# A decoder layer on one core: half of two transposed operands made by VectorE and DMAs, output projection by column halves

## The chip, the core and the metric

The kernel runs on one NeuronCore of a Trainium2 chip. A core has a matrix engine (TensorE, PE in the profile; its weight loads are PEld), VectorE (DVE), ScalarE (ACT), GpSimd (POOL) and SyncE (SP, which issues nearly all DMAs here), each with its own queue of instructions that run in order. The engines wait for each other through semaphores. The metric is the device time of one execution in microseconds.

## What is computed

One layer of a hybrid decoder on an input of 256 tokens by 1024 channels, float32, DEPTH and BATCH 1. Cut to what matters here:

```python
h = rmsnorm(x, norm1_g); u = h @ w_in            # split into x_rnn, g_rnn, q, k, v, g_br
ya = rg_lru(causal_dwconv(x_rnn)) * gelu(g_rnn)  # recurrent branch
yb = moba_attention(q, k, v)                     # 8 heads of 128; with 256 tokens: one causal block
gates = sigmoid(g_br)
merged = gates[0] * (ya @ w_proj_rnn) + gates[1] * (yb @ w_proj_attn)     # "the gated sum"
x = x + merged @ w_out
h = rmsnorm(x, norm2_g)
act = gelu(causal_dwconv(h @ w_up)) * (h @ w_gate)
x = x + act @ w_down
```

The products are made with three matmuls each: every operand is split into a high part (rounded to fp32r) and a low part (the rest), and hi*hi + hi*lo + lo*hi is summed in PSUM.

## The kernel before

**Weights as a stream.** All weights come as chunks of 128x2048 float32 (1 MB). `load_next` (L378) issues a chunk's DMA on SP into one of three raw buffers; `advance` (L401) loads up to three chunks ahead and has ScalarE make the high part (`hi`) and VectorE the low part (`lo`) with `split_part` (L397). For the chunks in `DVE_HI` (39, 42 and 43) VectorE makes both.

**Units.** `UNITS` (L34) lists the units of the first half of the layer. A unit takes one chunk: 4 quarters of 6 matmuls (`tm_mm`, L683: 2 halves of the tokens, 3 products), for half of the contraction and 512 output columns. So a pair of units, such as pa0 and pa1, makes 512 columns of one product, and the second one ends with the evacuation from PSUM. pr are the units of ya @ w_proj_rnn, pa of yb @ w_proj_attn, ga and gb of the gates. `pr_evac` (L843) multiplies with the gate, `pa_evac` (L847) multiplies and adds: half g (512 columns) of the gated sum then stands in `sgb`, tokens on the partitions.

**Transposes.** A product needs its stationary operand with the contraction on the partitions. `m_t` (L853) turns a quarter of the gated sum with four TensorE transposes (128x128, fp32) into PSUM and splits it into `mh`, `ml`; the four calls are the items m0 to m3. `norm2_t` (L949) does the same for a quarter of the updated x (one half of the tokens, one half of the columns; items n00, n10, n01, n11), multiplies with norm2_g and splits into `h2h`, `h2l`; it also sums the squares. The other way to transpose is `turn` (L437): VectorE transposes blocks of 32x32 within its partitions, four DMAs write the blocks to DRAM in the order in which they are to come back, and a fifth DMA, issued later as an item of its own, reads them. It is used for q, k, the recurrent branch and the FFN's up and gate products.

**Output projection.** `out_proj` (L968) uses `wout` in chunks of 256 rows by all 1024 columns; for each column half it runs over chunks, tokens and the two row blocks of a chunk (`rows_mm`, L933), 96 matmuls in four PSUM banks, and `norm2` (L945) adds the result to x in `xs`.

**FFN.** Blocks of 512 columns in pairs p = 0 to 4: `pair_half` (L1071) is a unit of 24 matmuls for up or gate and one half (kh) of the contraction. At the end of the second half the product is turned; `pair_up` and `pair_gate` work on it, and `downs` runs the down projection two pairs later. Pair 0's units come in the order up00, gt00, up01, gt01 (kind, pair, half of the contraction), the others' in the order up, up, gate, gate.

**The order.** Nothing is scheduled by the compiler. `AFTER` (L36) says after which quarter of which unit each item is put down. What the functions put down is kept in two lists, one for TensorE and one for all other engines, and `ORDER` (L161), a string written out in full, interleaves them: `+3` means the next three TensorE instructions, `157` the instruction with that number of the other list. The order of TensorE is fixed by the units; the order on every other queue, SP's too, by `ORDER`. Buffers are given out along this order (`Pool`, L245).

Of the kernel before, what the change touches and what calls it, by code (L numbers as in the profile page):

```python
# [14 lines left out]
P = 128  # L15
S = 256
D = 1024
KT = D // P
# [16 lines left out]
         "gb1 gb2 gb3 pr0 pr1 pr2 pr3 pa0 pa1 pa2 pa3")  # L35
# [65 lines left out]
    "pr2.1": "s36",  # L101
    "pr2.2": "O6",
    "pr2.3": "O0",
    "pr3.0": "s37",
    "pr3.3": "sb1",
    "pa1.0": "O7",
    "pa2.1": "m0",
    "pa3.2": "s38",
    "wo.0": "s39 m1",
    "wo.4": "m2",  # L110
    "wo.5": "s40",
    "wo.6": "m3",
    "wo.12": "n00",
    "wo.13": "n10",
    "wo.14": "s41",
    "up00.0": "s42 n01",
    "up00.2": "n11",
    "gt00.0": "s43",
    "gt00.3": "s44",
    "up01.3": "s45 s46",  # L120
    "gt01.2": "s47",
    "gt01.3": "bcast2",
    "up10.0": "ur0 s48",
    "up10.1": "s49",
    "up11.0": "s50",
    "up11.2": "fu0",
    "gt10.0": "s51",
    "gt10.1": "s52 gr0",
# [33 lines left out]
0-2 +1 3-4 +1 5 +1 6 +1 8 +1 7 +1 9 +1 11 +2 10 25 +1 12 30 +1 26-27 +1 14 +1 28 33 +1 29 +1 13 31 +2 32 +2 34 +1  # L162
35 +3 15 +7 36 +2 41 +3 19 +3 37 63 +1 42 +1 39 +3 43 +1 40 +1 17 38 +3 44 +1 49 +2 18 +3 45 64 50 +1 47 +4 51 46
+2 16 48 +3 52 +1 57 +4 53 +1 58 +1 55 +4 59 54 +2 56 +3 60 +7 66 +4 68 +1 67 +5 69 +3 99 +3 65 +5 70 100 +5 71 +5
72 +1 98 73 +1 74 +1 75 +1 76 +1 77 +1 78 104 +1 79-80 +1 81 +1 82 +1 83 +4 84 +1 105 +2 85 +4 116 +4 86 +1 103 +3
# [6 lines left out]
+6 188 228 +1 235 +4 189 +1 308 +2 242 190 +3 191 +2 162 240 +1 192 243 +2 244 247 +1 248 193 239 +1 249-250 +1  # L172
245 251 +2 246 +1 252 271 +2 272 +1 253 +1 229 +2 254 232 +1 309 +2 233 255 +2 230 +1 256 +2 322 +1 257 +2 231 +1
258 307 +2 234 +1 259 +3 260 273 +1 274-275 +1 276 108 261 +3 262 297 +2 323 +1 109 +1 263 329 +2 110 +3 277 +1
111 +3 112 +1 278 +6 299 279 +1 301 +1 321 +3 280 +2 332 330 +2 281 +3 282 +3 283 312 +2 311 302 +1 284 328 314 +2
264 313 305 285 +2 316 303 265 +1 286 315 +1 304 +1 317 +1 266 306 287 +1 318 +1 118 +1 288 +2 333 267 347 +1 289
+1 268 +2 194 269 +3 195 +2 298 196 +3 197 +1 300 +1 270 +1 198 +1 354 331 +1 355-356 +1 357 291 358 +3 290 359
# [8 lines left out]
+3 472 +1 391 +1 428 392 +1 393 +1 476 +3 478 +7 466 +1 473-474 467 +1 439 +2 468 +3 469 +1 527 470 +2 471 +5 484  # L186
+3 485 +2 479 +1 492 +3 494 +2 499 +6 486 528 +1 477 +3 496 +2 429 497 +2 537 +2 487 +1 539 +4 500 +3 507 +9 540
+1 502 498 +1 488 +1 503 +2 210 +1 489 +1 490-491 +2 431 +6 493 432 +4 495 +4 509 +2 510 +3 532 508 +12 504 538 +1
# [8 lines left out]
639 +3 655 +1 657 +9 668 653 +1 669-670 +1 671 +1 672 +1 673 +1 674 +1 675 +1 676 +1 658 +1 660 +9 677 +1 656 678  # L197
# [16 lines left out]
937 +1 936 +2 939 +1 938 +2 940-942  # L214
"""


class Ref:


    def __init__(self, make, root=None):
        self.make, self.made, self.root = make, None, root or self

# [76 lines left out]
def trunk_layer(ctx: ExitStack, tc: tile.TileContext, xT, x, vec, win_fm, win_tm, wri, wpr, wpa,  # L300
# [47 lines left out]
    def two(w, base, c):  # L348
# [7 lines left out]
              "pr": lambda c: two(wpr, 0, c), "pa": lambda c: two(wpa, 0, c)}  # L356
    units = [(u[:-1], int(u[-1])) for u in UNITS.split()]
    chunk = {u: add(source[u[0]](u[1])) for u in units}
    c_wo = [add(wout[c]) for c in range(4)]

    NP = NF // 2
    c_up, c_gt, c_dn = {}, {}, []
# [838 lines left out]
```

## Time and profile before

| | |
|---|---|
| median of 3 runs | 435.13 us (435.06 to 435.16) |
| the profiled execution | 435.01 us, its span 433.2 us |
| TensorE busy | 428.4 us (99%), 2044 instructions, granted clock 1.000 |
| VectorE, ScalarE, GpSimd busy | 326.8 (75%), 256.9 (59%), 50.1 us (12%) |
| DMA | 100.06 MB, mean 231 GB/s |

The span runs from the first to the last instruction; the rest of the profiled execution's time lies around it. In the profile's slices (40 equal parts of the span) a digit is a busy share in tenths. All operations carry line 296 (L296), the line at which the recorded list is issued, so the rows are told apart by their tiles: `mT` and `h2T` are the TensorE transposes of the gated sum and of x, `yo` the output projection, `sgb`, `xs`, `mh`, `ml`, `h2h`, `h2l` as above, `acc` the down projection, and names such as `fupd`, `gtm`, `gm`, `qm` are the SBUF and DRAM tiles of turns. "DMA to landing" is the time from the issue on SP to the last byte's semaphore.

### The profile page before, as it was taken

How to read it: one execution, taken by the hardware profiler on the slowest of the kernel's cores; microseconds unless marked ns; L12 is line 12 of the kernel's file. 1: busy time of each engine (PE TensorE's matmuls, PEld its weight loads, DVE VectorE, ACT ScalarE, POOL GpSimd, SP SyncE). 2: the span in 40 equal slices, each digit the busy share in tenths (PEclk: the TensorE clock that was granted, in tenths of full speed). 3: DMA queues.
4: the chain of work that ended last, by engine and by line, in shares of the span. 5: the costliest groups of instructions: out<-in, count | busy, mean ns of one | idle time of the engine just before them, and what ended most of it. 6: DMA issues, size and time to landing. Idle time of an engine off the chain costs nothing.

```text
span 433.2 us, 5466 instructions
## 1 busy us (share of the span) xinstructions
PE 428.4 (99%) x2044; PEld 360.0 (83%) x2044; DVE 326.8 (75%) x426; ACT 256.9 (59%) x285; POOL 50.1 (12%) x101
## 2 busy tenths in 40 slices
PE   8999999999999999999999999999999999999996
PEld 8888888888888888888888888888888888888985
DVE  3877499799888898985666896496979766767643
ACT  4687596886779999963431453357455555355410
POOL 0021007767660000000000000000000000000000
PEclk9999999999999999999999999999999999999999
DMA  7998944889991752274454466888789787697202
GB/s 259 404 385 243 360 153 147 269 292 326 372 358 52 276 194 97 98 290 130 163 194 141 151 220 202 288 288 300 238 264 328 256 285 245 211 317 249 97 2 97
DMA packets 32826, 100.06 MB, mean 231 GB/s; under 512 B 3104, under 2 KB 13472, under 8 KB 29088
## 3 DMA queue, kind: packets, MB, share of 16 engines
q1 hardware_dynamic: 32656, 99.71, 67.1%
q8 instruction: 16, 0.26, 0.2%
q14 instruction: 10, 0.08, 0.1%
q10 hardware_dynamic: 144, 0.00, 0.0%
HBM read 89.22 MB, written 10.49 MB: 230 GB/s over the span
## 4 chain that ended last, share of the span: by engine, by line
PE 97%; DMA 1%; DVE 0%; SPq 0%; ACT 0%; issue 0%
PE acc L296 14%; PE up L296 13%; PE gt L296 13%; PE pr L296 5%; PE gb L296 5%; PE yo L296 5%; PE ga L296 5%; PE v L296 5%; PE pa L296 5%; PE q L296 5%; PE k L296 5%; PE rg L296 5%; PE rx L296 4%; DMA raws<-in_win_fm 1%; PE gtl L296 1%; PE upl L296 1%
## 5 line engine op out<-in xcount | busy, mean ns | idle before, releaser
L296 DVE TENSOR_TENSOR lo<-raw,hi 128x2048 fp32r<-128x2048 f32 (+1 forms) x72 | 160.0, 2224 | 27.2 <-issue 9.5
L296 ACT CAST hi<-raw 128x2048 fp32r<-128x2048 f32 (+1 forms) x69 | 128.4, 1863 | 87.0 <-PE up L296 11.5
L296 PE MATMUL up<-hi,h2h 128*128 128x512 f32 x80 | 31.4, 393 | 0.0
L296 PE MATMUL up<-hi,h2l 128*128 128x512 f32 x80 | 31.1, 389 | 0.0
L296 PE MATMUL acc<-hi,fah 128*128 128x512 f32 x80 | 31.1, 389 | 0.0
L296 PE MATMUL acc<-lo,fah 128*128 128x512 f32 x80 | 31.1, 389 | 0.0
L296 PE MATMUL gt<-hi,h2l 128*128 128x512 f32 x80 | 31.1, 389 | 0.0
L296 PE MATMUL gt<-hi,h2h 128*128 128x512 f32 x80 | 31.1, 389 | 0.0
L296 PE MATMUL gt<-lo,h2h 128*128 128x512 f32 x80 | 31.1, 389 | 0.0
L296 PE MATMUL acc<-hi,fal 128*128 128x512 f32 x80 | 31.1, 389 | 0.0
L296 PE MATMUL up<-lo,h2h 128*128 128x512 f32 x80 | 31.1, 389 | 0.0
L296 ACT ACT_TABLE_LOAD x14 | 18.0, 1283 | 3.1 <-PEq L1191 1.2
L296 DVE SCALAR_TENSOR_TENSOR fc<-fu,pv,fc 128x255 f32<-128x255 f32 (+1 forms) x40 | 17.0, 475 | 2.0 <-ACT fc L296 1.9
L296 POOL TENSOR_TENSOR rsq<-rsq 128x8 f32<-128x8 f32 x32 | 17.1, 533 | 11.8 <-DVE rsq L296 9.6
L296 PEld LDWEIGHTS acc<-hi,fal 128*128 128x128 f32 x80 | 15.0, 188 | 3.2
L296 PEld LDWEIGHTS gt<-hi,h2h 128*128 128x128 f32 x80 | 15.0, 188 | 3.1
L296 PEld LDWEIGHTS up<-hi,h2l 128*128 128x128 f32 x80 | 15.0, 188 | 3.1
L296 PEld LDWEIGHTS acc<-hi,fah 128*128 128x128 f32 x80 | 15.0, 188 | 3.1
L296 PEld LDWEIGHTS gt<-lo,h2h 128*128 128x128 f32 x80 | 15.0, 188 | 3.1
L296 PEld LDWEIGHTS gt<-hi,h2l 128*128 128x128 f32 x80 | 15.0, 188 | 3.1
L296 PEld LDWEIGHTS up<-hi,h2h 128*128 128x128 f32 x80 | 15.0, 188 | 3.0
L296 PEld LDWEIGHTS acc<-lo,fah 128*128 128x128 f32 x80 | 15.0, 188 | 3.0
(228 smaller groups left out, 1041.3 us busy)
## 6 DMA issues: line engine op xcount, KB each, us to landing
raw<-in_win_fm SPq DMA_DIRECT2D x12, 1024.0 KB, 7.6
raw<-in_win_tm SPq DMA_DIRECT2D x12, 1024.0 KB, 6.2
raw<-in_wup SPq DMA_DIRECT2D x11, 1024.0 KB, 5.5
raw<-in_wgate SPq DMA_DIRECT2D x11, 1024.0 KB, 7.7
raw<-in_wdown SPq DMA_DIRECT2D x11, 1024.0 KB, 7.0
raw<-in_wpr SPq DMA_DIRECT2D x4, 1024.0 KB, 4.9
raw<-in_wpa SPq DMA_DIRECT2D x4, 1024.0 KB, 4.9
raw<-in_wout SPq DMA_DIRECT2D x4, 1024.0 KB, 4.8
```

The lines of the kernel that those rows point to most:

```text
L296: getattr(engine, name)(*map(real, a), **{n: real(v) for n, v in k.items()})
```

## The change

- Half 0 of the gated sum (columns 0 to 511) is turned with `turn` in place of m0 and m1: items mt (one VectorE transpose of 128x1024 and four writes), mr (the read), ms (cast and low part). m2 and m3 stay on TensorE.
- Half 1 of x for norm2 is turned in place of n01 and n11: ht (two VectorE transposes, four writes), hr (the read), hs (four ScalarE scalings by norm2_g, cast, low part, squares). n00 and n10 stay on TensorE.
- The output projection becomes four units wo0 to wo3 like the others: wo0 and wo1 make columns 0 to 511 over the whole contraction, wo2 and wo3 the rest. Each chunk is loaded by two DMAs of 512 KB.
- pa0 and pa1 run before pr3 (pr2, pa0, pa1, pr3, pa2, pa3), so half 0 of the gated sum is complete while three more units are left before wo0. Items of attention (O0, O6, O7) move with them.
- In the FFN the first units come as up00, gt00, up10, up01, gt01, up11, gt10, gt11: three units use half 0 of norm2's output before up01 needs half 1. Pair 1's products use the other PSUM pool.
- `ORDER` is written anew from near the start on, 958 numbers in place of 943 and 2015 TensorE instructions in place of 2031.

```diff
-         "gb1 gb2 gb3 pr0 pr1 pr2 pr3 pa0 pa1 pa2 pa3")
+         "gb1 gb2 gb3 pr0 pr1 pr2 pa0 pa1 pr3 pa2 pa3 wo0 wo1 wo2 wo3")
...
-    "pa1.0": "O7",
-    "pa2.1": "m0",
+    "pa0.0": "O6",
+    "pa0.2": "O7",
+    "pa1.0": "s37",
+    "pa1.3": "mt sb1",
+    "pr3.2": "mr",
+    "pa2.3": "ms",
...
-    "wo.0": "s39 m1",
-    "wo.4": "m2",
...
-    "wo.6": "m3",
-    "wo.12": "n00",
-    "wo.13": "n10",
...
-    "up00.0": "s42 n01",
-    "up00.2": "n11",
...
+    "wo0.1": "m2",
+    "wo0.2": "m3",
...
+    "wo2.0": "n00 s41",
+    "wo2.1": "n10",
+    "up00.0": "s42 ht",
+    "up00.3": "s43 hr",
+    "gt00.2": "hs",
...
+    def by_columns(w, c):
+
+        cs = slice(c // 2 * 512, c // 2 * 512 + 512)
+        return [w[2 * (c % 2) + j].rearrange("p (k c) -> p k c", k=2)[:, :, cs] for j in range(2)]
...
+            return [(n[:2], int(n[2]), int(n[3])) for n in "up00 gt00 up10 up01 gt01 up11 gt10 gt11".split()]
+        return [(kind, p, kh) for kind in ("up", "gt") for kh in range(2) if p > 1]
...
+    def m_turn():
+
+        turn("mm", turned_m, sgb.half(0), "mr")
...
+    def m_split():
+        v = lambda a: a.half(0).rearrange("p (u i b) -> p u i b", u=8, i=4)
+        split2(v(mh), v(ml), by_tile(turned_m))
+
+    def m_stat(a, k, t):
+        return head_q(a, k, t) if k < 4 else a[k][:, t * P:(t + 1) * P]
...
+    def norm2(hf, ps):
+        for t in range(2):
+            nc.vector.tensor_add(xs[:, t, halves[hf]], ps[t], xs[:, t, halves[hf]])
+
+    def squares(t, hf):
+        nc.scalar.activation(small(f"sq2{t}{hf}", 512), xs[:, t, halves[hf]], AF.Square,
+                             accum_out=ss2[:, hf, t:t + 1])
...
+    def h2_turn():
+        turn("hm", turned_h, [xs[:, t, halves[1]] for t in range(2)], "hr")
+
+    def h2_split():
+        m = half("h2p")
+        for k in range(4):
+            d = turned_h.rearrange("p (i t c b) -> p c t i b", i=4, t=2, c=4)[:, k]
+            nc.scalar.activation(kt(m)[:, k, :].rearrange("p (t i b) -> p t i b", t=2, i=4), d, AF.Copy,
+                                 scale=pv[:, V_G2 + 4 + k:V_G2 + 5 + k])
+        split2(h2h.half(1), h2l.half(1), m)
+        for t in range(2):
+            squares(t, 1)
...
-            open_ps[kind, p] = [bank(f"{kind}{p}{t}") for t in range(2)]
+            open_ps[kind, p] = [psA.tile([P, 512], F32, tag="A", name=f"{kind}{p}{t}") if p == 1 else bank(f"{kind}{p}{t}")
+                                 for t in range(2)]
```

More of the change, by code (lines that the diff above doesn't have):

```diff
@@ L100 @@
     "pr2.0": "P6",
[L101 to L105, printed above, removed]
-    "pa1.0": "O7",
-    "pa2.1": "m0",
-    "pa3.2": "s38",
-    "wo.0": "s39 m1",
-    "wo.4": "m2",
-    "wo.5": "s40",
-    "wo.6": "m3",
-    "wo.12": "n00",
-    "wo.13": "n10",
-    "wo.14": "s41",
-    "up00.0": "s42 n01",
-    "up00.2": "n11",
[L118 to L128, printed above, removed]
+    "pr2.1": "s36 O0",
+    "pa0.0": "O6",
[4 more added lines that the diff above has]
+    "pa2.3": "ms",
+    "pa3.2": "s38",
+    "wo0.0": "s39",
+    "wo0.1": "m2",
+    "wo0.2": "m3",
+    "wo1.0": "s40",
+    "wo2.0": "n00 s41",
[3 more added lines that the diff above has]
+    "gt00.2": "hs",
+    "up10.0": "s44 s45",
+    "up01.0": "s46 bcast2",
+    "gt01.0": "s47",
+    "up11.0": "s48 ur0",
+    "gt10.0": "s49 s50",
+    "gt10.2": "s51 fu0",
+    "gt11.0": "s52 gr0",
     "gt11.1": "ur1",
@@ L161 @@
 ORDER = """
[L162 to L165, printed above, removed]
[6 rows of a table removed]
-+6 188 228 +1 235 +4 189 +1 308 +2 242 190 +3 191 +2 162 240 +1 192 243 +2 244 247 +1 248 193 239 +1 249-250 +1
@@ L173 @@
[L173 to L177, printed above, removed]
[8 rows of a table removed]
@@ L186 @@
-+3 472 +1 391 +1 428 392 +1 393 +1 476 +3 478 +7 466 +1 473-474 467 +1 439 +2 468 +3 469 +1 527 470 +2 471 +5 484
-+3 485 +2 479 +1 492 +3 494 +2 499 +6 486 528 +1 477 +3 496 +2 429 497 +2 537 +2 487 +1 539 +4 500 +3 507 +9 540
-+1 502 498 +1 488 +1 503 +2 210 +1 489 +1 490-491 +2 431 +6 493 432 +4 495 +4 509 +2 510 +3 532 508 +12 504 538 +1
[8 rows of a table removed]
-639 +3 655 +1 657 +9 668 653 +1 669-670 +1 671 +1 672 +1 673 +1 674 +1 675 +1 676 +1 658 +1 660 +9 677 +1 656 678
[16 rows of a table removed]
-937 +1 936 +2 939 +1 938 +2 940-942
+0-2 +1 3-4 +1 5 +1 6 +1 8 +1 7 +1 9 +1 11 +2 10 25 +1 12 30 +1 26-27 +1 14 +1 28 33 +1 29 +1 13 31 +2 32 +2 34 +2
@@ new lines @@
+35 +3 15 +6 36 +3 41 +3 19 +2 37 +1 63 42 +1 39 +4 43 38 +1 17 +1 40 +3 44 +1 49 +4 45 64 +1 50 +1 47 18 +3 51 +1
+46 +1 16 +1 48 +2 52 +2 57 +4 53 +1 58 +1 55 +3 59 +1 54 +1 56 +3 60 +8 66 +4 68 67 +6 69 +2 99 +3 65 +5 70 +1 100
++10 104 98 +8 71 105 +10 72 +1 103 73 +1 116 74 +1 75 +1 76 +1 77-78 +1 79 +1 80 +1 81 +1 82 +2 117 +3 61 137 +4
[7 rows of a table added]
++1 235 +3 204 +2 308 +2 242 +1 205 +4 247 206 240 +1 248 239 +1 249-250 +1 243 251 +1 244 +2 252 245 +2 246 +1 253
[4 rows of a table added]
++2 270 +1 209 +3 298 +3 300 +3 331 +1 354 +1 355-356 +1 357 290 358 +3 291 359 326 +2 348 +1 320 360 327 +3 350
[8 rows of a table added]
@@ L215 @@
+392 +1 393 +1 469 +1 470-471 +2 472 538 +1 210 +3 473 +3 484 +3 485 +2 479 +2 492 +2 494 +3 499 +5 486 539 +1 477
[10 rows of a table added]
+671-672 +1 673 +1 674 664 +1 666 +8 650 +1 675 +1 659 676 +1 677 662 +1 678 +1 679 +1 680 +1 681-682 +8 667 +4 651
[16 rows of a table added]
+952 +1 951 +2 954 +1 953 +2 955-957
 """
@@ L355, in trunk_layer, with ffn_order @@
               "ga": lambda c: two(win_fm, 8, c), "gb": lambda c: two(win_fm, 12, c),
-              "pr": lambda c: two(wpr, 0, c), "pa": lambda c: two(wpa, 0, c)}
+              "pr": lambda c: two(wpr, 0, c), "pa": lambda c: two(wpa, 0, c), "wo": lambda c: by_columns(wout, c)}
     units = [(u[:-1], int(u[-1])) for u in UNITS.split()]
     chunk = {u: add(source[u[0]](u[1])) for u in units}
-    c_wo = [add(wout[c]) for c in range(4)]
     NP = NF // 2
+    def ffn_order(p):
+        if p == 0:
+            return [(n[:2], int(n[2]), int(n[3])) for n in "up00 gt00 up10 up01 gt01 up11 gt10 gt11".split()]
+        return [(kind, p, kh) for kind in ("up", "gt") for kh in range(2) if p > 1]
     c_up, c_gt, c_dn = {}, {}, []
     for p in range(NP):
-        for c, kh in ((c_up, 0), (c_gt, 0), (c_up, 1), (c_gt, 1)) if p == 0 else (
-                (c_up, 0), (c_up, 1), (c_gt, 0), (c_gt, 1)):
+        for kind, p, kh in ffn_order(p):
+            c = c_up if kind == "up" else c_gt
             c[p, kh] = add(two(wup if c is c_up else wgate, 0, 2 * p + kh))
@@ L381, in load_next @@
         raw[i] = wp.tile([P, 2048], F32, tag="raw", name=f"raw{i}")
+        if isinstance(stream[i], list):
+            n = 2048 // len(stream[i])
+            for a, src in enumerate(stream[i]):
+                d = raw[i][:, a * n:(a + 1) * n]
+                nc.sync.dma_start(d.rearrange("p (k c) -> p k c", k=2) if len(src.shape) == 3 else d, src)
+            return
         if len(stream[i].shape) == 3:
@@ L405, in advance @@
             j = split_tiles()
-            n, m = min(2048, stream[j].shape[-1] * (2 if len(stream[j].shape) == 3 else 1)), {4: 2}.get(j, 1)
+            src = stream[j]
+            n = 2048 if isinstance(src, list) else min(2048, src.shape[-1] * (2 if len(src.shape) == 3 else 1))
+            m = {4: 2}.get(j, 1)
             for a in range(m):
@@ L681, in trunk_layer, with tm_mm @@
     ybh, ybl = Act("ybh", F32R), Act("ybl", F32R)
-    def tm_mm(ps, i, k, k4, ah, al, split=False):
+    def tm_mm(ps, i, k, k4, ah, al, split=False, stat=lambda a, k, t: a[k][:, t * P:(t + 1) * P]):
         at = (lambda a: a.rearrange("p (c k n) -> p k c n", c=2, k=4)[:, k4]) if split else (
@@ L688, in tm_mm @@
         for t in range(2):
-            ts = slice(t * P, (t + 1) * P)
             o = ps[t].rearrange("p (c n) -> p c n", c=2) if split else ps[t]
-            mm3(o, ah[k][:, ts], al[k][:, ts], at(hi[i]), at(lo[i]), k == 0, k == KT - 1)
+            mm3(o, stat(ah, k, t), stat(al, k, t), at(hi[i]), at(lo[i]), k == 0, k == KT - 1)
     SC = P ** -0.5
@@ L851, in pa_evac, with by_tile @@
             nc.vector.tensor_add(m, m, tok(sga, g, t))
+    turned_m = half("md")
+    def m_turn():
+        turn("mm", turned_m, sgb.half(0), "mr")
+    def by_tile(d):
+        return d.rearrange("p (i u b) -> p u i b", u=8, i=4)
+    def m_split():
[3 more added lines that the diff above has]
+        return head_q(a, k, t) if k < 4 else a[k][:, t * P:(t + 1) * P]
     def m_t(c):
@@ L862, in trunk_layer @@
     evac = {"rg": rg_ps.__setitem__, "v": v_evac, "pr": pr_evac, "pa": pa_evac, "ga": lambda g, ps: gate_evac(sga, g, ps),
-            "gb": lambda g, ps: gate_evac(sgb, g, ps)}
+            "gb": lambda g, ps: gate_evac(sgb, g, ps), "wo": lambda g, ps: norm2(g, ps)}
     def run_unit(kind, c):
@@ L897, in run_unit @@
             for k4 in range(4):
-                tm_mm(ps, i, 4 * kh + k4, k4, *{"pr": (yah, yal), "pa": (ybh, ybl)}.get(kind, (xgh, xgl)),
-                      kind not in "qkv")
+                tm_mm(ps, i, 4 * kh + k4, k4, *{"pr": (yah, yal), "pa": (ybh, ybl), "wo": (mh, ml)}.get(kind, (xgh, xgl)),
+                      kind not in ("q", "k", "v", "wo"), *((m_stat,) if kind == "wo" else ()))
                 if kh and k4 == 3:
@@ L917, in trunk_layer @@
             item[f"{n}{h}"] = lambda fn=fn, h=h: fn(h)
-    for n in range(4):
+    for n in (2, 3):
         item[f"m{n}"] = lambda n=n: m_t(n)
+    item["mt"], item["ms"] = m_turn, m_split
     def run(name, quarters):
@@ L925, in run @@
                 advance(int(n[1:])) if n[1:].isdigit() and n[0] == "s" else item[n]()
-    yo = {}
     h2h, h2l = Act("h2h", F32R), Act("h2l", F32R)
@@ L943, in trunk_layer @@
     rs2 = const.tile([P, 2], F32, name="rs2")
-    def norm2(t, hf):
-        cs = halves[hf]
-        nc.vector.tensor_add(xs[:, t, cs], yo[t, hf], xs[:, t, cs])
+    def norm2(hf, ps):
[4 more added lines that the diff above has]
+                             accum_out=ss2[:, hf, t:t + 1])
+    turned_h = half("hd")
+    def h2_turn():
[9 more added lines that the diff above has]
+            squares(t, 1)
     def norm2_t(t, hf):
@@ L958, in norm2_t @@
         split2(kt(h2h.half(hf))[:, :, ts], kt(h2l.half(hf))[:, :, ts], m)
-        nc.scalar.activation(small(f"sq2{t}{hf}", 512), xs[:, t, halves[hf]], AF.Square,
-                             accum_out=ss2[:, hf, t:t + 1])
-    def wo(j, t, hf):
-        advance(c_wo[j])
-        if j == 0:
-            yo[t, hf] = psA.tile([P, 512], F32, tag="A", name=f"yo{t}{hf}")
-        rows_mm(yo[t, hf], c_wo[j], mh.pair(j), ml.pair(j), t, halves[hf], j == 0, j == 3)
-    def out_proj():
-        for hf in range(2):
-            for j in (0, 1):
-                for t in range(2):
-                    wo(j, t, hf)
-                    yield
-        for hf in range(2):
-            for t in range(2):
-                wo(2, t, hf)
-                yield
-                wo(3, t, hf)
-                norm2(t, hf)
-                yield
+        squares(t, hf)
     for t in range(2):
-        for hf in range(2):
-            item[f"n{t}{hf}"] = lambda t=t, hf=hf: norm2_t(t, hf)
+        item[f"n{t}0"] = lambda t=t: norm2_t(t, 0)
+    item["ht"], item["hs"] = h2_turn, h2_split
     for kind, c in units:
@@ L987, in trunk_layer @@
             run(f"{kind}{c}", run_unit(kind, c))
-    run("wo", out_proj())
     rbf = const.tile([P, S], F32, name="rbf")
@@ L1067, in trunk_layer @@
         item[f"fg{p}"] = lambda p=p: pair_gate(p)
-    item["n11"] = lambda: norm2_t(1, 1)
     item["bcast2"] = norm2_bcast
@@ L1107, in trunk_layer @@
     for p in range(NP):
-        for kind, kh in (("up", 0), ("gt", 0), ("up", 1), ("gt", 1)) if p == 0 else (
-                ("up", 0), ("up", 1), ("gt", 0), ("gt", 1)):
-            run(f"{kind}{p}{kh}", pair_half(kind, p, kh))
+        for kind, n, kh in ffn_order(p):
+            run(f"{kind}{n}{kh}", pair_half(kind, n, kh))
         if p >= 2:
```

83 rows, old and new, of the table ORDER are left out of this document.

## The prediction

> **What bounds the kernel now.** I read the page first: its shares, its slices and the chain that ended last.
>
> ```profile
> span 433.2 us, 5466 instructions
> ...
> PE 428.4 (99%) x2044; PEld 360.0 (83%) x2044; DVE 326.8 (75%) x426; ACT 256.9 (59%) x285; POOL 50.1 (12%) x101
> ...
> PE   8999999999999999999999999999999999999996
> ...
> DMA  7998944889991752274454466888789787697202
> ...
> PE 97%; DMA 1%; DVE 0%; SPq 0%; ACT 0%; issue 0%
> ```
>
> TensorE is busy in 9 tenths or more of every slice but the first and the last, and 97% of the chain is TensorE. The view of TensorE's waits says how little is lost to others:
>
> ```profile
> PE warm L296 <- DVE ones L296: 1.0, 1, 1.0
> PE rx L296 <- ACT his L296: 0.2, 1, 0.2
> ```
>
> 1.2 us, both before the stream is running. So from about 10 us on the time is the sum of TensorE's instructions. Removing one saves what it takes in the queue; any new wait of TensorE is added in full. The chain in order of time (start, length, what) gives these prices:
>
> ```profile
> 225.35 0.44 PE mT L296 x4
> ...
> 249.47 0.44 PE h2T L296 x4
> 249.90 2.74 PE up L296 x12
> 252.65 0.44 PE h2T L296 x4
> 253.08 1.38 PE up L296 x6
> 254.46 5.44 PE gt L296 x24
> ```
>
> A group of four transposes takes 0.44 us; a unit (24 matmuls with 512 columns) takes 5.44 us, 0.227 us per matmul. Quoted are three of the four groups that the change removes (m1, n01, n11); m0's takes the same.
>
> **The change part by part.**
>
> *Transposes removed from TensorE:* 4 groups x 0.44 = 1.76 us. The matmul after a group starts some hundredths late as well (249.90 with 12 matmuls takes 2.74, against 12 x 0.2267 = 2.72), so I take 0.45 a group: 1.80 us. All of it is on the path. Listed singly, a transpose is longer:
>
> ```profile
> L296 PE MATMUL h2T<-ident,xs 128*128 128x128 f32 x16 | 2.4, 272 | 0.0
> ```
>
> 272 ns is the time of one from start to end (mT's are the same), and they overlap: 0.44/4 = 0.11 us each is what they hold the queue for, and that is what I take. [...]
>
> *Output projection by column halves:* 4 units of 24 matmuls, 96 as before, of the same shape. Nothing on TensorE. Its loads become 8 of 512 KB instead of 4 of 1024 KB: four more issues on SP. In the new order each such load stands 87 to 117 matmuls (20 to 27 us) ahead of use, against 4.8 us from issue to landing now:
>
> ```profile
> raw<-in_wout SPq DMA_DIRECT2D x4, 1024.0 KB, 4.8
> ```
>
> No gain is possible, and a load four times as slow would still be in time: nothing.
>
> *The work of the two turns.* Durations, VectorE first, then ScalarE:
>
> ```profile
> L296 DVE STREAM_TRANSPOSE qd<-q 128x512 f32<-128x512 f32 x4 | 2.7, 698 | 0.0
> L296 DVE TENSOR_TENSOR h2l<-h,h2h 128x512 fp32r<-128x512 f32 x4 | 2.7, 690 | 0.9 <-ACT h2h L296 0.7
> ...
> L296 DVE STREAM_TRANSPOSE kd<-kr 128x1024 f32<-128x1024 f32 x2 | 2.5, 1242 | 0.0
> ...
> L296 DVE TENSOR_TENSOR qTl<-qd,qTh 128x1024 fp32r<-128x1024 f32 x2 | 2.5, 1232 | 1.1 <-ACT qTh L296 1.1
> ```
>
> ```profile
> L296 ACT ACTIVATE fc<-fu,pv 128x256 f32<-128x256 f32 x20 | 10.7, 593 | 6.2 <-DVE fu L296 6.2
> ...
> L296 ACT ACTIVATE qTh<-qd 128x1024 fp32r<-128x1024 f32 x2 | 2.1, 1046 | 0.0
> ```
>
> VectorE loses six instructions of 128x512 (two each of ml, h and h2l), 6 x 0.69 = 4.1 us, and gets 1.24 + 2 x 0.70 (transposes) + 2 x 1.23 (low parts) = 5.1 us; ScalarE gets 4 x 0.59 + 2 x 1.05 for four casts of about 0.6, some 2 us more. VectorE is 75% busy, so one more microsecond is covered. What matters is the latency: VectorE transposes, four DMAs write to DRAM, one reads back, then ScalarE and VectorE split. The nearest rows for an uncrowded round trip (issues on SP; then KB and us to landing, each from its own window):
>
> ```profile
> 86.17 1.78 SPq L296 DMA_DIRECT2D gm<-gr  x4
> ```
>
> ```profile
> gm<-gr SPq DMA_DIRECT2D x4, 128.0 KB, 2.4
> ```
>
> ```profile
> raw<-in_wri SPq DMA_DIRECT2D x1, 512.0 KB, 3.2
> ```
>
> Last write issued about 1.4 us after the first, landed 2.4 later, then a 512 KB read of 3.2: 7.1 us with a little for semaphores. The crowded end is the FFN:
>
> ```profile
> 268.25 2.39 SPq L296 DMA_DIRECT2D upm<-fupd  x4
> ```
>
> ```profile
> upm<-fupd SPq DMA_DIRECT2D x4, 128.0 KB, 5.7
> ```
>
> ```profile
> fupd<-upm SPq DMA_DIRECT2D x1, 512.0 KB, 6.3
> ```
>
> Some 1.8 us between first and last issue, 5.7 and 6.3: 13.8 us. I take 7.1 for both new turns, because in the new order the last weight load stands 16 to 28 matmuls (4 to 6 us) ahead of the writes, near its landing, and the next one behind the read.
>
> *First turn (half of the gated sum).* Call T0 the end of unit pa1. How long the sum takes after it, from VectorE's timeline:
>
> ```profile
> 211.97 1.37 DVE L296 TENSOR_TENSOR sgb<-pa,sgb 128x512 f32<-128x512 f32 x2 [2.65 <-PE pa L296]
> 213.26 1.28 DVE L296 TENSOR_TENSOR sgb<-sgb,sga 128x512 f32<-128x512 f32 x2
> ```
>
> It ends at 214.54. The chain, in the same stretch:
>
> ```profile
> 208.45 6.89 PE pa L296 x30
> ```
>
> The first 18 of these 30 are the end of pa1, so pa1 ended near 212.6: the sum is there at T0+1.9. Transposed T0+3.1, landed T0+10.3. The order puts two low-part splits, two multiplies and the cast and low part of wo1 on VectorE in between; at about 2.3, 0.7, 1.2 and 2.3 us they run until T0+12.5, so the low part is ready by T0+13.7. TensorE has three units (pr3, pa2, pa3) before wo0: T0+16.3, and wants the low part at the third matmul, T0+16.8. Spare: 3.1 us. At the crowded price it would be ready at T0+19.5: a stall of 2.7 us. Behind the waiting cast stand ScalarE's casts of wo2 and wo3, behind the waiting read SP's loads of the same chunks, used two units later.
>
> *Second turn (half of norm2's input).* T1 is the end of wo3. The last addition into xs ends at about T1+0.9, the two transposes at T1+2.3, the round trip at T1+9.5 (SP can issue at once: its load of gt01 is issued before T1, when VectorE has split gt00). Then four scalings, cast and low part: 2.4 + 1.05 + 1.23 and 0.2 of semaphores = 4.9, ready T1+14.4. Between lie three units (up00, gt00, up10): up01 starts at T1+16.3 and wants the low part at 16.8. Spare: 2.4 us; crowded price: a stall of 4.3 us. Behind the waiting first scaling stands ScalarE's cast for up11, and behind the waiting read SP's loads of up11 and gt10; they are due two to four units later.
>
> *Attention units inside the recurrent branch's, pair 1 opened early, the written order renewed.* The count of matmuls for attention is the same. In the stretch of the projections the low parts of the weights stand 34 to 69 matmuls ahead of use in the new order, 19 to 63 before (wo1 apart): easier. P6 and O0 stay well ahead of pa0 (the last low part of yb0 10 matmuls, 2.3 us, for a 0.42 us instruction). PSUM: pair 1 uses the four banks that wo frees. Cost nothing; bounds, by the 0.2 us wait at the start that could vanish or double, and by a few hundredths where transposes of attention change neighbours: -0.2 to +0.3 us.
>
> **Sum.** The profiled execution took 435.01 us, 1.8 of it outside its span; minus 1.80 gives 433.2. The median of the runs is 0.12 higher: 433.3 us.
>
> **The rivals.**
>
> *A turn comes late (the other side).* If the second round trip is crowded like the FFN's, TensorE waits 4.3 us at up01.0: 435.1 - 1.8 + 4.3 = 437.6 us. It decides from a round trip of 9.5 us on (stall begins) and 11.3 us (gain gone). For it: the quoted read of 6.3 us, which shared the queue with weights and other turns. Against: DMA is at 4 to 6 tenths here (the 19th to 24th slice), at 6 to 9 in the FFN. [...] Chance 0.11.
>
> *Half late.* A crowded write (7.5) with a free read (3.2) is 10.7 us, a stall of 1.2 us: 434.5, within 0.2% of before. Chance 0.10.
>
> *The FFN's DMA burst.* In the new order up of pair 0, gate of pair 0 and up of pair 1 finish in three units running (now two, and the third after a gap), so 1 MB more crowds the queue at one place. Tightest today, VectorE's timeline and the chain:
>
> ```profile
> 367.25 2.29 DVE L296 TENSOR_TENSOR lo<-raw,hi 128x2048 fp32r<-128x2048 f32 x1
> ```
>
> ```profile
> 369.18 10.88 PE gt L296 x48
> ```
>
> The low part ends at 369.54 and its unit starts at 374.6: 5.1 us spare where SP has already been held up. A megabyte more is about 3.2 us: twice the difference between the quoted 4.8 for 1024 KB and 3.2 for 512 KB. Covered; if not, a stall of 1 to 2 us, 434.3 to 435.3. Chance 0.04, half of it slower or same.
>
> *Each transpose holds TensorE for its listed 272 ns:* 16 x 0.272 = 4.35 us, 430.8. The chain speaks against. 0.02.
>
> *The removed time does not come back* because what follows was waiting anyway: the waits view shows none. In the same 0.10 as half late.
>
> **How the numbers follow.** Clean gain 0.73, with its own range 432.9 to 433.8 (the bounds above). 0.2% is 0.87 us, about what a measurement tells from no change. Faster (below 434.26): 0.73 + 0.02 + 0.02 = 0.77; same 0.10 + 0.01 = 0.11; slower 0.12. Range 432.7 to 435.2: up to where the gain is just lost, which leaves out the late turn and the 272 ns case.
>
> **What would show it.** Right: TensorE's waits still two lines before 11 us; the chain without mT before pa's last unit and with two h2T groups; wo in units of 5.44 us; the first scaling behind the turn on ScalarE ends several microseconds before up of pair 0 starts its second half. Wrong: a wait of PE wo on the low part of the gated sum, or of PE up on h2l; a wait of PE on lo anywhere in the FFN; the round trips longer than 9.5 us.

## The result and the profile after

| | before | after |
|---|---|---|
| median | 435.15 us (434.94 to 435.6, 8 runs) | 437.18 us (434.93 to 438.63, 8 runs) |
| profiled execution, its span | 435.01, 433.2 us | 438.48, 436.7 us |
| TensorE busy, instructions | 428.4 us, 2044 | 428.0 us, 2028 |
| ScalarE busy, table loads | 256.9 us, 14 | 262.0 us, 17 |

The changed kernel is slower: 1.0046 times the time of before, interval 1.0032 to 1.0061, some 2.0 us. Forecast were 433.3 us, a gain of 1.8. Sixteen TensorE instructions are gone, and TensorE's busy time has hardly fallen. The page of after shows the place. In the lines with slices each digit is a fortieth of the span, 10.9 us.

```profile
span 436.7 us, 5470 instructions
...
PE 428.0 (98%) x2028; PEld 359.7 (82%) x2028; DVE 328.8 (75%) x425; ACT 262.0 (60%) x290; POOL 50.3 (12%) x101
...
PE   8999999999988999999999999999999999999996
...
PEclk9999999999998999999999999999999999999999
...
PE 86%; DMA 6%; ACT 4%; DVE 2%; issue 1%; SPq 0%; ACTq 0%
```

Two slices of TensorE show an 8 in the middle of the kernel (the 12th and 13th, 120 to 142 us), the granted clock dips in the 13th, and the chain that ended last, 97% TensorE before, now runs 14% of the way through other engines. The place is the attention stage, 80 us ahead of the first of the new turns. TensorE's waits (in all, times, longest) name the wait:

```profile
PE pt L293 <- DVE sm L293: 3.5, 1, 3.5
PE warm L293 <- DVE ones L293: 1.0, 1, 1.0
PE rx L293 <- ACT his L293: 0.8, 1, 0.8
```

`pt` are the TensorE transposes of a head's softmax `sm`; this is the first head that is worked on. The chain in order of time shows what they waited for:

```profile
131.04 1.18 ACT sm L293 x4
...
132.44 0.30 DVE sm L293
...
132.88 0.88 PE pt L293 x3
133.75 6.52 PE ga L293 x24
```

ScalarE's exponentials came late, and VectorE scaled them at once. Behind the wait, 24 matmuls of `ga` took 6.52 us. The windows of that stretch (length, then busy time and count for each engine, granted clock, DMA share, GB/s) show why:

```profile
128.50:133.00 4.50, 1.01 (x8) 0.80 (x7) 2.05 (x8) 4.47 (x9) 1.87 (x6) 0.94 0.79 252
133.00:136.50 3.50, 3.50 (x12) 2.88 (x13) 3.33 (x9) 3.50 (x7) 0.00 (x0) 0.59 0.70 253
```

For 3.5 us after the wait the granted clock is 0.59: a loss of 3.5 x 0.41 = 1.4 us more, with which the idle time is paid for a second time. "Busy" hides it, since slow matmuls count as busy.

**The balance.** The first `pt` transposes start at 132.88, against 128.84 before:

```profile
128.84 0.33 PE pt L296 x3
129.17 5.51 PE ga L296 x24
```

That is 4.04 us late, some 0.5 of it from the start of the kernel (the wait of `rx` for the first weights, 0.8 against 0.2 us in the waits view) and the rest from the wait. The 0.5 is not the work of the new order: the first load took 6.69 us in place of 6.19, and the two orders are the same up to TensorE's 20th instruction. In the runs below the wait of `rx` was anything from none (old front) to 1.0 us (casts of q and k back). At the lower clock the transposes take 0.88 in place of 0.33 and the matmuls 6.52 in place of 5.51, together 1.6 us. That makes 5.6 us, and from there on nothing is lost. At the end of the changed stretch (gate of pair 0; before it began at 254.46, a row of the prediction) the lag is 258.13 - 254.46 = 3.67 us:

```profile
242.22 0.44 PE h2T L293 x4
...
252.69 5.44 PE up L293 x24
258.13 5.44 PE gt L293 x24
263.57 6.81 PE up L293 x30
```

So 0.5 + 3.5 + 1.6 us came in ahead, and 5.6 - 3.7 = 1.9 us were taken off in the stretch where the four groups of transposes stood. The gain came as forecast; it is hidden by a loss elsewhere. The mean granted clock was 0.999 or 1.000 in three of the eight runs (434.93 to 436.13 us) and 0.992 to 0.996 in the other five (437.17 to 438.63 us), so the second payment is not made in every execution.

**Why the exponentials were late.** ScalarE before, from its timeline (start, length, instruction, in brackets the idle time ahead of it and what ended it):

```profile
121.25 1.06 ACT L296 ACTIVATE tt<-rt 128x1024 f32<-128x1024 f32 x1 [2.12 <-DVE rt L296]
123.19 1.28 ACT L296 ACT_TABLE_LOAD   x1 [0.87 <-DVE mx L296]
124.48 0.49 ACT L296 ACTIVATE sm<-sm,mx,rq 128x128 f32<-128x128 f32 x1
```

and after:

```profile
111.53 1.06 ACT L293 ACTIVATE qTh<-qd 128x1024 fp32r<-128x1024 f32 x1 [5.25 <-DMA qd<-qm]
...
113.88 1.90 ACT L293 CAST hi<-raw 128x2048 fp32r<-128x2048 f32 x1
...
119.04 1.28 ACT L293 ACT_TABLE_LOAD   x1
120.33 1.06 ACT L293 ACTIVATE rt<-rt 128x1024 f32<-128x1024 f32 x1
121.43 1.06 ACT L293 ACTIVATE a<-rt 128x1024 f32<-128x1024 f32 x1
122.39 1.04 ACT L293 ACTIVATE tt<-rt 128x1024 f32<-128x1024 f32 x1
123.47 1.06 ACT L293 ACTIVATE rt<-rt 128x1024 f32<-128x1024 f32 x1
...
127.38 1.28 ACT L293 ACT_TABLE_LOAD   x1
128.68 1.06 ACT L293 ACTIVATE tt<-tt 128x1024 f32<-128x1024 f32 x1
129.74 1.28 ACT L293 ACT_TABLE_LOAD   x1
131.04 0.49 ACT L293 ACTIVATE sm<-sm,mx,rq 128x128 f32<-128x128 f32 x1
```

Before, ScalarE idles for 0.87 us and is there when the softmax's maximum `mx` is ready. After, the renewed order has put the recurrent branch's elementwise work (`rt`, `a`, `tt`) ahead of the softmax: five more activations of 1.06 us ahead of the first softmax and two more table loads (three in place of one), since exponential, square root and the softmax's exponential follow each other. Between these rows stand a weight cast and a cast of the turned k of 1.1 us, which had its place behind the softmax before. It also put the casts of the turned q and k ahead of a weight cast (`hi` of ga2), so ScalarE sat idle for 5.25 us until the read of q landed, and from there on it had no time left. Two suspects, then, and a third: the DMAs of the turns had also changed places.

**The new turns.** Their rows, SP's issues first, then ScalarE, then VectorE:

```profile
215.95 1.79 SPq L293 DMA_DIRECT2D mm<-md  x4
...
254.66 1.78 SPq L293 DMA_DIRECT2D hm<-hd  x4
```

```profile
223.03 1.05 ACT L293 CAST mh<-md 128x1024 fp32r<-128x1024 f32 x1 [8.37 <-DMA md<-mm]
...
262.54 1.71 ACT L293 ACTIVATE h2p<-hd,pv 128x256 f32<-128x256 f32 x4 [2.45 <-DMA hd<-hm]
```

```profile
225.61 1.22 DVE L293 TENSOR_TENSOR ml<-md,mh 128x1024 fp32r<-128x1024 f32 x1
...
265.65 1.22 DVE L293 TENSOR_TENSOR h2l<-h2p,h2h 128x1024 fp32r<-128x1024 f32 x1
```

First turn: pa1 ended at 212.7 (T0; the chain's next piece, pr3, starts at 212.71), from the first write to the cast 7.1 us, low part ready at 226.8 = T0+14.1 (forecast 13.7). Second: wo3 ended at 252.7 (T1), 7.9 us, ready at 266.9 = T1+14.2 (forecast 14.4); up01's third matmul came at about 269.5. Spare 2.6 us where 2.4 was forecast, and no wait.

### The profile page after: what moved, and what is told of

Read it like the earlier page. It is cut to its first block, busy times and chain, and to the rows that moved or that the text cites. A ratio compares the mean times of both kernels' runs of the same rounds, so it can differ in the third digit from the quotient of the medians.

```text
span 436.7 us, 5470 instructions
## 1 busy us (share of the span) xinstructions
PE 428.0 (98%) x2028; PEld 359.7 (82%) x2028; DVE 328.8 (75%) x425; ACT 262.0 (60%) x290; POOL 50.3 (12%) x101
## 4 chain that ended last, share of the span: by engine, by line
PE 86%; DMA 6%; ACT 4%; DVE 2%; issue 1%; SPq 0%; ACTq 0%
PE acc L293 13%; PE up L293 12%; PE gt L293 12%; PE gb L293 5%; PE pr L293 5%; PE wo L293 5%; PE pa L293 5%; PE k L293 5%; PE rg L293 5%; PE rx L293 4%; PE v L293 3%; PE q L293 2%; DMA raw<-in_win_tm 2%; DMA kd<-km 2%; PE ga L293 2%; DMA raws<-in_win_fm 2%
## 5 line engine op out<-in xcount | busy, mean ns | idle before, releaser
L293 ACT ACT_TABLE_LOAD x17 | 21.8, 1283 | 3.5 <-DVE fc L293 2.2
L293 POOL TENSOR_TENSOR rsq<-rsq 128x8 f32<-128x8 f32 x32 | 18.4, 576 | 31.8 <-DVE rsq L293 29.6
L293 PEld LDWEIGHTS up<-lo,h2h 128*128 128x128 f32 x80 | 15.0, 188 | 3.1
```

Of the source, the lines that this page charges most:

```text
L293: getattr(engine, name)(*map(real, a), **{n: real(v) for n, v in k.items()})
```

## The experiments

**Theory A**, from the two traces: the loss is in the renewed order of the first part alone, and it is ScalarE's recurrent work (with the idle time ahead of the turned q) in front of the first softmax. **Rivals:** the reads or writes of the turns at new places on SP (B); the casts that wait for them (C); the change itself costs more than the wait shows (D).

**Old front, new rest; and new front, old rest.** `ORDER` of the one kernel up to the end of unit gb3 (TensorE instruction 832), of the other behind it:

```diff
 # changed kernel, old front
-ORDER: all numbers as in the change
+ORDER: up to TensorE instruction 832 as before, behind it as in the change
 # kernel before, new front
-ORDER: all numbers as before
+ORDER: up to TensorE instruction 832 as in the change, behind it as before
```

> The changed kernel with the order of before up to the end of the gates' units (TensorE instruction 832), from there on its own order; nothing else differs. If the loss sits in the renewed order of the attention stage (TensorE waiting 3.5 us for the first head's softmax, then 1.1 us at a lower clock), the wait is gone and the four removed groups of transposes remain: 435.15 - 1.8 = 433.3 us, granted clock 1.00, no wait of PE pt. If the loss came from the change proper (turns, column halves, pair 1 early) and only shows at the softmax, the time stays at 436 to 438.

> The kernel before with the changed kernel's order up to TensorE instruction 832, its own order behind it: no turn of the gated sum or of norm2's input, all 32 transposes on TensorE. If the renewed order of the front is the cause, it shows the same wait at the first softmax and is the changed kernel plus the 1.8 us of transposes: about 439 us (436.7 to 440.5, as the wait varies from run to run). If the change proper is the cause: 435.2.

Measured: the changed kernel with the old front takes 433.18 us (432.64 to 433.44), 0.996 of before [0.9948, 0.9972]. TensorE waits for nothing but the first load:

```profile
PE warm L291 <- DVE ones L291: 1.0, 1, 1.0
```

and its chain has, where the lag was read above,

```profile
252.28 5.44 PE gt L291 x24
```

Gate of pair 0 begins 2.18 us earlier than before (254.46); some 0.3 of that is a shorter start. Against the kernel before in the same measurement (434.84 us) the gain is 1.7 us. The kernel before with the new front takes 438.92 us (438.66 to 439.79), 1.0098 [1.0085, 1.0111], with the wait and the clock dip:

```profile
PE pt L294 <- DVE sm L294: 2.5, 1, 2.5
```

The loss lies in the front and the gain behind it, and D falls. The version with the old front is the fastest of all; its 433.18 us are 0.1 from the forecast.

**The turns' DMAs back** (39 entries of `ORDER` get another place: SP's writes, reads and loads of the attention stage and VectorE's turn of the gate, at the places of before).

```diff
-"gm" turned after TensorE instruction 379, read at 617; qm, km written, read and loads in between as in the change
+"gm" turned after TensorE instruction 470, read at 542; the others at the places of before
```

> The changed kernel with the DMAs of the attention stage (loads, writes and reads of the turns) and the two transposes of the gate's turn where before has them; ScalarE's and VectorE's other work as in the changed kernel. Theory of the late reads: reads of q and k are back about 3 us earlier, no wait, 433.3 us. Theory of the queues: with the recurrent branch still ahead of the softmax there is no spare time; the wait shrinks by what the reads gain but varies from run to run, 434 to 437.

Measured: 438.61 us (437.28 to 439.77), ratio 1.0088 [1.0074, 1.0103], above even the 437 that I had set as the upper end, and the wait is all there:

```profile
PE pt L291 <- DVE sm L291: 3.7, 1, 3.7
```

B falls: q was read earlier (its cast starts at 108.77 in place of 111.53), yet the first exponential, at 130.69 in place of 131.04, hardly moved, as ScalarE still had to wait for k and then do the recurrent work.

**The recurrent work behind the softmax** (nine instructions; the softmax's first exponential stands at 561).

```diff
 # place: TensorE instructions ahead of it
-exp, square of half 0 (ScalarE) 518, 523; tanh, exp of half 1 527, 532; square root of half 0 551; square of half 1 622
+exp, square of half 0           598, 606; tanh, exp of half 1 640, 648; square root of half 0 628; square of half 1 660
-multiplies of half 0 and 1 (VectorE) 525, 540, 545
+multiplies of half 0 and 1           594, 614, 600
```

> The changed kernel with nine instructions of the recurrent branch (tanh, two exp, two squares, sqrt on ScalarE; three multiplies on VectorE) put behind the first head's softmax instead of ahead of it; the DMAs' order is the changed kernel's. Theory of the queues: ScalarE reaches the first exp about 6 us earlier and VectorE the first maximum 3 us earlier, no wait of PE pt, 433.3 us. Theory of the late reads (the turns of q and k return 3 us later than before, and that alone makes the wait): the reads stay late, a wait of 1 us or more stays, 435 or more.

Measured: 436.1 us (435.48 to 436.53), 1.0033 [1.002, 1.0046], clock 1.000. The wait of 3.5 us is gone, but others have come:

```profile
PE pt L291 <- DVE sm L291: 0.8, 2, 0.5
PE pa L291 <- ACT ybh L291: 0.5, 1, 0.5
```

The two of `pt` belong to later heads (their transposes start at 139.71 and 178.86 us), the wait of `pa` ends at 196.85. In all, TensorE reaches `wo` 2.5 us later than with the old front, beside a start that is 0.3 longer. For the first of these waits the trace points to a reason: on VectorE the three moved multiplies (1.22 us each; two of `it` at 129.12 and 131.45, one of `tt` at 135.37) now stand between the heads, and the softmax in question is scaled at 139.37. The old front makes the two of `it` at 104.3 and 107.6, and scales this softmax at 135.42. The other two waits were not separated. So this edit takes away the first wait and pays for it elsewhere: the old front is better than this mend.

**The casts of the turned q and k back** (C).

```diff
-cast of q 486, its low part 491; cast of k 491, low part 496; cast of ga2's weights 495
+cast of q 492, its low part 497; cast of k 508, low part 513; cast of ga2's weights 484
```

> The changed kernel, with five instructions back at the places of before: ScalarE's casts and VectorE's low parts of the first turned q and k, and ScalarE's cast of the weights of ga2, which then stands ahead of the turned q again instead of behind it. The recurrent branch's work stays ahead of the first softmax. In the changed kernel ScalarE sat idle for 5.25 us ahead of the turned q (until 111.53) and then worked without a gap until the first exponential at 131.04. Theory (length of ScalarE's queue, both parts count): the 1.9 us cast of ga2 goes into the idle gap, everything behind it comes 1.9 us earlier, the wait at the first transposes of the softmax falls from 3.5 to 1.6 us, the granted clock stays at 1.0, and the time is near 434.3 (434 to 435). Rival 1 (the casts waiting for the reads are the whole cause): the wait is gone and the time is 433.2 to 433.5. Rival 2 (only the recurrent branch's work counts): wait 3.5 us, time 437.

Measured: 436.54 us (434.83 to 438.03, 6 runs), 1.0036 [1.0017, 1.0055]. In the profiled execution the span is 434.0 us, the clock 1.000 and the wait

```profile
PE pt L291 <- DVE sm L291: 2.2, 1, 2.2
```

So 1.3 us of the wait come from that idle gap, and the rest stays. I had expected 1.9: the weight cast fills the gap, but the next instruction then waits 1.92 us for VectorE. Three of the six runs had a mean clock of 0.995 or 0.996 (436.81 to 438.03 us). The three at 1.000 took 434.83 to 436.28 us, so the clock is not all that lies above the expected 434.3; the profiled execution also has a start that is 0.6 us longer than with the old front. C alone falls; as a part it holds.

**Both edits together.** The diff is the sum of the two above.

> The changed kernel with both edits: the casts of the first turned q and k and of ga2 at the places of before, and the nine instructions of the recurrent branch behind the first softmax. Theory: the first exponential starts near 121.5 and there is no wait at its transposes; what is left against the version with the whole old front (433.2) are the smaller waits that the moved recurrent work causes later (0.5 and 0.3 us at two other heads' transposes, 0.5 us at unit pa in the run with that edit alone): 435 to 436. Rival (those smaller waits came of ScalarE's idle gap too): they vanish, and the time is 433.2 to 433.7.

Measured: 436.49 us (435.9 to 438.83), 1.0042 [1.0022, 1.0062], somewhat above the expected 435 to 436; the first exponential starts at 122.62, and its wait is gone. The smaller waits are much the same as in the run with the recurrent work moved alone (0.9 us for `pt` in two, 0.6 for `pa`; there 0.8 and 0.5), so they don't come of ScalarE's idle gap.

**The recurrent work alone, in the kernel before.** The last run asks whether it is enough.

```diff
 # kernel before; the first softmax's maxima stand at 556 and 558, its exponential at 562
-exp, square of half 0 620, 641; VectorE's multiply 680; tanh, exp of half 1 652, 666; square root of half 0 686
+exp, square of half 0 556, 556; VectorE's multiply 557; tanh, exp of half 1 558, 559; square root of half 0 560
```

> The kernel before, with nothing of the change but this: six instructions of the recurrent branch (ScalarE's exponential and square of half 0, tanh and exponential of half 1, square root of half 0, and the one VectorE instruction between them) are put ahead of the first softmax. Theory (recurrent work on ScalarE ahead of the first softmax is enough by itself): five instructions of 1.06 us and two more table loads of 1.28 us are 7.9 us, of which some 2 us fall into ScalarE's idle time; the first exponential starts near 130.3 instead of 124.48, its transposes are ready near 132.3 and TensorE wants them at 128.84. Wait of 3.4 us, then a lower granted clock for some 3.5 us (1.1 us more): 4.9 us longer than before, 439.8 us (438 to 440.5). Rival (the wait needs the new places of the turns' casts or of the DMAs as well): no wait or one under 1 us, 435 to 436.

Measured: 441.15 us (440.68 to 442.56), 1.0149 [1.0132, 1.0166].

```profile
PE pt L294 <- DVE sm L294: 4.3, 1, 4.3
```

```profile
122.50 1.28 ACT L294 ACT_TABLE_LOAD   x1
...
131.65 0.49 ACT L294 ACTIVATE sm<-sm,mx,rq 128x128 f32<-128x128 f32 x1
```

```profile
133.00:136.50 3.50, 3.02 (x9) 2.56 (x10) 3.18 (x14) 3.50 (x4) 0.00 (x0) 0.50 0.46 159
136.50:140.00 3.50, 3.50 (x10) 2.73 (x10) 1.89 (x9) 3.50 (x8) 0.00 (x0) 0.59 0.00 0
```

Six instructions in a kernel of 5466 cost 6.6 us: the wait is 0.9 us longer than expected (the exponential comes 1.3 us later, since the idle time that could take up the work was the 0.87 us of the row of before, not 2 us), and the clock stays low for 6.83 us, about twice the 3.5 expected. Theory A stands: this work ahead of the first softmax is enough, and taking it away is what removes the wait.

**The price of the removed transposes.** In the version with the old front, each of norm2's two groups of transposes is done three times, 16 instructions more:

```diff
-        for k4 in range(4):
+        for k4 in 3 * list(range(4)):
             k = 4 * hf + k4
             nc.tensor.transpose(ps[:, k4, :], xs[:, t, k * P:(k + 1) * P], ident)
```

> The changed kernel with the old front, and 16 transposes more on TensorE: each of the two groups of four that norm2 has left is done three times into the same bank. That is the number that the change removed, with nothing else given back. By the chain's 0.44 to 0.45 us a group: 1.8 us more than the version with the old front (433.2), so 435.0 us, the time of the kernel before. Rival (a transpose holds TensorE for its listed 272 ns): 4.35 us more, 437.5. Rival (a group hides beside something): no change.

Measured: 434.69 us (434.31 to 435.39, 11 runs), 0.9999 [0.999, 1.0008]. The chain:

```profile
236.32 1.31 PE h2T L291 x12
```

12 transposes take 1.31 us (the second group of norm2 the same), so eight more cost 0.87 and a group 0.44. The span is 1.7 us longer than without them (432.5 against 430.8). The 272 ns of one would have given 4.35.

**The spare of the second turn.** In the version with the old front the read that ends the second turn is done three times in series:

```diff
-        item[read] = lambda: nc.sync.dma_start(dst, mid)
+        item[read] = lambda: [nc.sync.dma_start(dst, mid) for _ in range(3 if read == "hr" else 1)]
```

> The changed kernel with the old front, and the read that ends the second turn (half of norm2's input) done three times in series, the last two for nothing. One read took 3.6 us in the version with the old front, so the low part is ready some 7.0 us later. There it was ready at 261.0, and TensorE wanted it at about 263.5: spare 2.5 us. Theory: a stall of 4.5 us in unit up01, and if a wait of TensorE of that length is followed by a lower granted clock here too (0.59 for 3.5 us after the wait of 3.5 us in the changed kernel), 1 us more: 437.5 to 439. Rival (the spare is larger than my bookkeeping says): a stall under 3 us, 433.5 to 436. Rival (what stands on SP behind the waiting reads comes late as well): further waits in up11 or gt10, over 440.

Measured: 439.99 us (438.64 to 442.86, 4 runs), 1.0123 [1.0091, 1.0155]. TensorE's waits, and the windows around them:

```profile
PE up L291 <- ACT h2h L291: 3.4, 1, 3.4
...
PE up L291 <- DVE h2l L291: 0.5, 1, 0.5
```

```profile
267.50:270.00 2.50, 1.97 (x8) 1.39 (x7) 1.92 (x2) 1.32 (x1) 0.00 (x0) 0.78 0.96 303
270.00:272.50 2.50, 2.50 (x9) 2.11 (x9) 1.15 (x1) 2.17 (x2) 0.00 (x0) 0.54 0.72 254
```

3.9 us of waits, where 4.5 was expected from a spare of 2.5: the spare was there. The clock then costs 2.5 x 0.22 + 2.5 x 0.46 = 1.7 us, where I had allowed 1. Together that is 5.6 us against 5.5, so it does not explain why the median lies above my range. The profiled span is 6.9 us above that of the old front (437.7 against 430.8): 0.5 of the rest is a longer start, and 0.8 stays open. Two of the four runs had a mean clock of 0.990 and 0.992, lower than the 0.994 of the profiled one; they are the two slowest. In the profiled execution nothing queued behind the read came late: there is no third wait.

## Why the prediction was wrong

The step that failed is "the written order renewed", with "Cost nothing; bounds [...] -0.2 to +0.3 us". It cost 5.1 us in the profiled execution, 3.5 for the wait at the first softmax and 1.6 for the clock behind it (the 0.5 in the start is no part of it). By the medians, each against the kernel before in its own measurement, it cost 3.7 us: the changed kernel was 2.0 slower, with the old front 1.7 faster. For that step I weighed the lead of the weights' low parts, of O0, P6 and pa0, and PSUM, and thought of the attention only as a count of matmuls. I never asked how early the first softmax is ready. The profile before had the answer. VectorE's timeline:

```profile
125.89 0.55 DVE L296 TENSOR_SCALAR sm<-sm,mx 128x128 f32<-128x128 f32 x2
```

The scaled softmax is there at 126.44, and TensorE takes it at 128.84. That is a spare of 2.4 us, as small as that of the turns on which I spent most of the working, and the order written anew put five ScalarE instructions of 1.06 us and two table loads of 1.28 us ahead of it. The rival for the other side named the right kind of event (a late operand on TensorE in place of the one expected early) at the wrong place: the chance 0.11 stood on the second turn, and none on the front.

Point by point:

- TensorE as the bound, each wait of it paid in full: right, and too mild. A wait of 3.5 us cost 1.6 us more, as the granted clock fell to 0.59 over the 3.5 us behind it.
- Transposes, 0.45 us a group, 1.80 in all: right (about 1.9 between two rows of the traces, 0.44 a group in the chain of the run that adds eight to each group). The 272 ns case is excluded.
- Output projection by column halves at nothing: right, no wait at `wo` in any run.
- First turn: round trip 7.1 us forecast and measured, low part 0.4 us later than forecast, no wait. Second turn: 7.9 in place of 7.1, low part 0.2 us earlier, no wait. The spare of 2.4 held under test.
- The FFN's burst: no wait of `up` or `gt` on `lo`.
- The sum for all but the failed step: 433.3 forecast, 433.18 measured with the old front; as a gain over the kernel before 1.8 forecast, 1.7 measured. The clean case's own range of 432.9 to 433.8 does not follow from its bounds (-0.2 and +0.3 on 433.3 give 433.1 to 433.6); nothing else rests on it.

## What to carry to other kernels

When a change comes with a new order, every consumer that waits in order behind other work is part of the change: list the operands that TensorE takes, with their spare in the profile before, over the whole kernel and not only where the new operations stand. An engine with 60% busy time on average can be the bound of one stage (ScalarE here, busy for 4.47 of the 4.50 us around the wait); elementwise work that nobody waits for goes behind the work on the critical operand, above all where it switches activation tables (1.28 us a load here), but into a stage that has room for it: moved just behind the first softmax it made other waits here (0.8 us of `pt`, 0.5 us of `pa`), which at the old places it did not. Where a kernel at 99% busy becomes slower, TensorE's waits and the clock row point to the place, and the order cut in two there tells its halves apart.

## What was not expected of the hardware

- In the five profiled executions with a wait of TensorE of 2.5 us or more, the granted clock then was 0.50 for 3.41 us, in one of them (the recurrent work alone, wait 4.3 us) for 6.83 us; the figures between 0.5 and 1 in the rows above come of windows that cover the edge of such a stretch. At half the clock, 3.41 us cost 1.7 us, and 1.7 us are 0.004 of the span: a mean clock of 0.996 fits one such stretch, 0.992 two (the profiled execution with 6.83 us reads 0.991). After a wait of 2.2 us the profiled execution kept 1.00, and half of that kernel's runs, whose waits are not traced, did not. After waits of 0.5 and 0.6 us alone (the recurrent work moved, and both edits) the profiled executions kept 1.00.
- Each change of activation tables took 1.28 us on ScalarE (17 loads, 21.8 us, against 14 and 18.0 before), more than an activation of 128x1024 with its 1.06.
- The wait's length alone does not tell what the clock did. By the waits, the windows and the mean clocks of the profiled executions:

| run | TensorE's wait | it ends at | granted clock falls to 0.50 at | and stays there for |
|---|---|---|---|---|
| changed kernel | 3.5 us | 132.9 us | 132.4 us | 3.4 us |
| before, new front | 2.5 us | 130.7 us | 132.2 us | 3.4 us |
| turns' DMAs back | 3.7 us | 132.5 us | 134.0 us | 3.4 us |
| second turn slowed | 3.4 and 0.5 us | 268.3 us | 268.9 us | 3.4 us |
| recurrent work alone | 4.3 us | 133.5 us | 132.6 us | 6.8 us |
| casts of q and k back | 2.2 us | 131.4 us | does not fall | none |

The wait of 3.7 us was followed by no more time at half clock than the one of 2.5 us, and the fall came up to 1.5 us behind the wait's end or up to 0.9 us ahead of it. What decides whether and when the clock falls was not shown.
